# Retention's output projection as seven block products in a written order, with its row and weight sums made during the gates

## The chip, the cores and the metric

One Trainium2 chip, of which the kernel uses one core. The metric is the device time of one execution in microseconds (us), the median of three runs. In the profiled execution TensorE had 0.998 of its full clock granted, so times can be compared across the whole span.

## The reference, cut to what matters

One layer of a backbone over 1024 tokens and 1024 channels, all in float32: a modulated norm, one wide input projection, neighbourhood attention and bidirectional retention side by side, two sigmoid gates that merge the two branches, an output projection, then a gated MLP. The change is in the retention branch's own projection, in the merge and in what stands next to them:

```python
def _ret_output(o, g):
    ...
    return _merge_heads(on) * jax.nn.silu(g)

def _merge(o_na, o_ret, gate_na, gate_ret, w_proj_na, w_proj_ret, w_out):
    merged = jax.nn.sigmoid(gate_na) * (o_na @ w_proj_na) + jax.nn.sigmoid(gate_ret) * (o_ret @ w_proj_ret)
    return merged @ w_out
```

`o_ret` has 1024 tokens and 1024 columns, `w_proj_ret` is 1024 by 1024. The product `o_ret @ w_proj_ret` is what is computed in another way.

## The kernel before, in words

**Three matmuls for one.** Every float32 operand is split into a high and a low part (`split`, L92): ScalarE casts the tile to the high part (L93), VectorE subtracts that from the tile to get the low part (L94). A product is then three matmuls, high by high, high by low and low by high (`mm_a`, `mm3`, L117 to L130, or `open3`, L1420). So each weight tile of 128 by 512 costs one load, one ScalarE cast and one VectorE subtraction before TensorE can use it. Weights are loaded by SyncE's queue into `raw` buffers, of which there are three (L97), and split into `wc` buffers, of which there are six.

**Seven products.** The gate projections, the MLP's up and the MLP's down projection already use Strassen-Winograd's seven products in place of eight (`Seven`, L1424): both operands are cut in 2 by 2 blocks (A11 to A22 for the weights, B11 to B22 for the rows), four sums of each side are made (S1 to S4, T1 to T4), and the seven products are collected in PSUM and combined on VectorE. The sums of the weights come from one of two places: they are made in DRAM, by copies and accumulating DMAs that GpSimd's queue issues long ahead (`block_sums`, L553, pulled a few at a time by `puts`), or by four `tensor_tensor` adds on GpSimd when the unit is loaded (`Seven.load`, L1427). For the up projection `PRE` (L550) is the number of units whose sums are made in DRAM: 8 before. The others, which come later, add on GpSimd.

**The stages around the change,** in the time of the profile: the gates (to about 891 us; class `Gates`, the unit of one head or one merge gate, its steps interleaved by `interleaved`); the retention projection (891.3 to 978.3 us); the output projection `out_proj` (L1707, from 978.3 us), whose eight token tiles multiply the merged rows with `w_out`; and the up projection of the MLP (units `Opening`, `Later` and `Up`).

**The gates leave their rows in DRAM.** For a retention head, `Gates.done` (L1528) takes Silu of the gate, multiplies it with the normed retention output (L1533) and stores the tile to `d_orr` (L1534). For a merge gate it stores the sigmoid to `d_gate` and the gated attention branch to `d_pn`.

**The retention projection** loads the sixteen `orr` tiles (eight of 128 rows for each half of the tokens) and splits them (`orr_load`, `orr_split`). `pret(db, half)` (L1659) then makes one output tile of 128 channels by 512 tokens: 8 k-blocks by 3 matmuls into one PSUM bank `pr`; VectorE multiplies it with the gate (`sg`, L1663, which reads PSUM); GpSimd adds the attention branch (L1664; VectorE for the last `db`); ScalarE and VectorE split the sum into `mh` and `ml` for the output projection. There are 8 `db` by 2 halves, so 16 such tiles and 384 matmuls. After the loop come the loads and splits of `w_out` (`wo`, L1692, and `wx`/`wc`, L1705).

**What sets the order.** All of this stands in code that a scheduler may move: it orders each engine's instructions itself. Inside `with tc.manual_schedule()` the written order holds on each engine.

Of the kernel before, what the change touches and what calls it, by code (L numbers as in the profile page):

```python
# [8 lines left out]
F32 = mybir.dt.float32  # L9
# [31 lines left out]
def tile_hybrid_layer(ctx, tc: tile.TileContext, io, dbg=None):  # L41
# [25 lines left out]
    d_w = dram.tile([NF // 2, 4, P, 512], F32, name="d_w")  # L67

# [481 lines left out]
    NH, EARLY, PRE = NF // 2, 4, 8  # L550
# [25 lines left out]
    def gate_jobs():  # L576
        return weight_jobs(d_g, [io["w_rg"][h] for h in range(RH)] + [io["w_gate"][db] for db in range((NA_FILL + RET_FILL) // 2, KB)])

    def up_jobs():
        return weight_jobs(d_s, [io["w_up"][seq[n]] for n in range(PRE)])  # L580
# [11 lines left out]
    gate_sums, up_sums = block_sums(gate_jobs()), block_sums(up_jobs())  # L592
# [793 lines left out]
    def g_raw(name):  # L1386
        return rr.tile([P, 512], F32, tag="r", bufs=10, name=name)
# [95 lines left out]

    class Gates(Seven):
# [43 lines left out]
        def done(self, b, half, t=None, src=None):  # L1528
            t = self.c[b, half]
            src, n, cs = t if src is None else src, self.n, slice(half * 512, half * 512 + 512)  # L1530
            act.activation(t, src, AF.Silu if self.kind == "ret" else AF.Sigmoid)
            if self.kind == "ret" or b == 0:
                vec.tensor_tensor(t, t, self.o, ALU.mult)  # L1533
                pool.dma_start(d_orr[2 * n + b, :, cs] if self.kind == "ret" else d_pn[n, half], t)  # L1534
            else:
                act.dma_start(d_gate[2 * n + 1, half], t)

# [60 lines left out]
    orr = {}  # L1598

    def orr_load(raw, half, k, pin=late):  # L1600
        pin(sync.dma_start(raw, d_orr[k, :, half * 512 : half * 512 + 512]))
        return half, k, raw

    def orr_split(half, k, raw):
        i, kb = (k // KH if half else 1 - k // KH), k % KH + KH * half
        orr[half, k] = [hxpool.tile([P, 512], F32R, tag=f"{t}{i}{kb}", bufs=1, name="orr") for t in ("high", "low")]
        split(*orr[half, k], raw)

    steps = interleaved(0, len(gu))
    n0, fetched = steps.index((len(gu) - 1, 0)), []  # L1610
    for n, (i, k) in enumerate(steps):
        gu[i].step(k)
        if k in (1, 2, 3):
            puts(up_sums, (gu[i].u3 if k == 3 else gu[i].u2)[:, 0:1], 2)
        if len(fetched) > 1:
            orr_split(*fetched.pop(0))
        if n0 - KH - 1 <= n < n0 - 1:
            fetched.append(orr_load(wpool.tile([P, 512], F32, tag="raw", bufs=3, name="raw"), 0, n - n0 + KH + 1))
        elif n0 < n <= n0 + KH:
            fetched.append(orr_load(g_raw("orw"), 0, n - n0 - 1 + KH))  # L1620

    def pret_load(db):
        return [wload(io["w_pret"][db, i]) for i in range(2)]

    for r in fetched:
        orr_split(*r)
    wp = {0: pret_load(0)}
# [12 lines left out]

    def merge_load(db, halves=(0, 1)):
        for half in halves:
            sg[db, 0, half] = gtile(half, F32, "sg")
            sync.dma_start(sg[db, 0, half], d_pn[db, half])
            sg[db, 1, half] = t = gtile(half, F32, "sg")
            sync.dma_start(t, d_gate[2 * db + 1, half])
            if (db, 1) in spilled:
                act.activation(t, t, AF.Sigmoid)

# [6 lines left out]

    mg = {}

    def pret(db, half):  # L1659
        m = g_ps("pr")  # L1660
        mm_a(m, wp[db], lambda k: orr[half, k][0], lambda k: orr[half, k][1])
        g = sg[db, 1, half]
        vec.tensor_tensor(g, m, g, ALU.mult)  # L1663
        (vec if db == KB - 1 else pool).tensor_tensor(g, g, sg[db, 0, half], ALU.add)  # L1664
# [5 lines left out]
    merge_load(0, (0,))  # L1670
    rows = [orr_load(gtile(1, F32, "orw"), 1, k, lambda ins: ins) for k in range(2 * RH)]
    for r in rows:
        orr_split(*r)
    wp[1] = pret_load(1)
    merge_load(1, (0,))
    for half in range(2):
        if half:
            merge_load(0, (1,))
            merge_load(1, (1,))
        for db in range(2):  # L1680
            pret(db, half)
    for db in range(2, KB):
        wp[db] = pret_load(db)
        merge_load(db)
        if db == 2:
            brow(0, gate1)
        for half in range(2):
            pret(db, half)
    wo = {}
    for kb in range(KB):  # L1690
        t = wop.tile([P, 2, 512], F32R, tag="wo", bufs=KB, name="wo")
        wo[kb, 0] = wload(io["w_out"][0, kb], into=t)  # L1692
# [10 lines left out]
    for kb in (6, 7, 0, 1, 2, 3, 4, 5):  # L1703
        t = (wop if kb >= 6 else op).tile([P, 2, 512], F32R, tag="wx", bufs=2, name="wx") if kb >= 4 else None
        wo[kb, 1] = wload(io["w_out"][1, kb], into=t)  # L1705
# [237 lines left out]

    opening = [Opening(n) for n in range(EARLY)]
    o0, o1, o2, o3 = opening
    xr = None
    for tb in range(NTB):
# [8 lines left out]
        nx = out_proj(tb)  # L1956
# [398 lines left out]
```

## Time and profile before

| what | value |
| --- | --- |
| median of three runs | 1713.74 us (1713.53 to 1713.92) |
| the profiled execution's own time | 1713.59 us |
| its span, first to last instruction | 1711.8 us (1.8 us lie outside it) |
| VectorE busy | 1224.5 us, 72% |
| ScalarE busy | 832.1 us, 49% |
| GpSimd busy | 595.0 us, 35% |

How to read it: the page gives the busy time of each engine over the whole span, and these shares are averages over stages with different limits. So the views that count here are those cut to a stage: busy time by windows, groups of instructions in a window, and the timeline of one engine. DVE is VectorE, ACT ScalarE, POOL GpSimd, PE TensorE, SP SyncE. In a row of the timeline the first number is the start in us, the second the duration; a row with `x2` stands for two instructions run back to back. In a row of a tile the three numbers between slashes are the shortest, median and longest duration in ns.

### The profile page before, as it was taken

What the parts mean: (1) busy time and instruction counts of PE and PEld (TensorE: products, weight loads), DVE (VectorE), ACT (ScalarE), POOL (GpSimd) and SP (SyncE); (2) the same over time, 40 slices, a digit from 0 to 9 for tenths busy, and PEclk for the clock granted to TensorE, in tenths of its full rate; (3) what the DMA queues carried; (4) which work ended last, traced back from release to release, by engine and by line L of the source; (5) the groups of instructions that cost most, each with busy time, mean ns of one, the idle gap of its engine ahead of it and who ended that gap; (6) DMA issues with size and microseconds to landing.
All of it is one profiled execution on the core that took longest, in us unless ns stands there. A gap on an engine that the chain in (4) does not pass through costs nothing.

```text
span 1711.8 us, 25236 instructions
## 1 busy us (share of the span) xinstructions
PE 1696.4 (99%) x8413; PEld 1418.8 (83%) x8413; DVE 1224.5 (72%) x2423; ACT 832.1 (49%) x1749; POOL 595.0 (35%) x783
## 2 busy tenths in 40 slices
PE   9999999999999999999999999999999999999998
PEld 7788888888888887888888888888888888888886
DVE  5777786665787777565564556897899889846756
ACT  6665665553454435353453323654444444634444
POOL 2112324322344443023322111013666567311444
PEclk9999999999999999999999999999999999999999
DMA  9256779952353533899995657878667766998744
GB/s 378 95 147 170 175 202 233 217 132 63 108 145 93 173 62 91 268 309 308 308 288 175 219 175 209 284 228 251 167 169 199 191 186 174 272 312 288 244 157 176
DMA packets 167554, 344.01 MB, mean 201 GB/s; under 512 B 29824, under 2 KB 46752, under 8 KB 160832
## 3 DMA queue, kind: packets, MB, share of 16 engines
q1 hardware_dynamic: 131888, 242.40, 41.6%
q0 software_dynamic: 20928, 85.06, 23.2%
q10 hardware_dynamic: 14608, 14.95, 2.6%
q8 instruction: 66, 1.08, 0.2%
q14 instruction: 64, 0.52, 0.1%
HBM read 267.03 MB, written 140.82 MB: 238 GB/s over the span
## 4 chain that ended last, share of the span: by engine, by line
PE 81%; DMA 5%; issue 5%; DVE 4%; POOL 3%; ACT 1%; SPq 0%; POOLq 0%; ACTq 0%; DVEq 0%
PE u L1417 31%; PE mm L130 4%; PE mm L128 4%; PE mm L129 4%; PE mm L118 4%; PE mm L119 4%; PE mm L117 4%; PE y L1417 2%; PE R L520 2%; PE ptp L502 2%; DMA ur<-in_w_down 2%; PE pr L118 2%; PE pr L117 2%; PE pr L119 2%; DMA ur<-d_a 2%
## 5 line engine op out<-in xcount | busy, mean ns | idle before, releaser
L1417 PE MATMUL u<-T,wc 128*128 128x512 f32 x1056 | 246.4, 389 | 0.3 <-DVE T L94 0.2
L1417 PEld LDWEIGHTS u<-T,wc 128*128 128x128 f32 x1056 | 198.0, 188 | 42.4 <-DVE T L94 0.6
L1417 PE MATMUL y<-wc,ahl 128*128 128x512 f32 (+1 forms) x936 | 210.1, 386 | 0.4 <-DVE wc L94 0.4
L1417 PEld LDWEIGHTS y<-wc,ahl 128*128 128x128 f32 x936 | 174.1, 188 | 36.4 <-DVE wc L94 0.8
L94 DVE TENSOR_TENSOR wc<-ur,wc 128x512 fp32r<-128x512 f32 x171 | 126.8, 745 | 49.0 <-ACT wc L93 49.0
L93 ACT CAST wc<-ur 128x512 fp32r<-128x512 f32 x171 | 105.7, 622 | 110.4 <-PE u L1417 57.1
L118 PE MATMUL mm<-low,wc 128*128 128x512 f32 (+1 forms) x312 | 119.1, 382 | 0.0
L1417 PE MATMUL u<-h2a,wc 128*128 128x512 f32 x504 | 118.3, 389 | 0.0
L1417 PEld LDWEIGHTS u<-h2a,wc 128*128 128x128 f32 x504 | 94.5, 188 | 19.6
L117 PE MATMUL mm<-hx,wc 128*128 128x512 f32 x264 | 107.2, 406 | 0.3 <-ACT hc L231 0.3
L119 PE MATMUL mm<-hx,wc 128*128 128x512 f32 x264 | 104.8, 397 | 0.0
L532 POOL DMA_DIRECT2D d_ona<-rs x32 | 32.5, 1014 | 207.7 <-DVE st L493 55.0
L1417 PE MATMUL u<-hxT,wc 128*128 128x512 f32 x384 | 90.0, 389 | 0.0
L588 POOL COPY pad<-pu 128x1 f32<-128x1 f32 x62 | 39.7, 640 | 143.0 <-DVE pu L1458 107.1
L1417 PEld LDWEIGHTS u<-hxT,wc 128*128 128x128 f32 x384 | 72.1, 188 | 15.0
L130 PE MATMUL mm<-wc,low 128*128 128x512 f32 (+1 forms) x180 | 68.9, 383 | 0.0
L93 ACT CAST wc<-s 128x512 fp32r<-128x512 f32 x56 | 34.9, 623 | 69.6 <-PE u L1417 65.3
L94 DVE TENSOR_TENSOR ahl<-ur,ahl 128x512 fp32r<-128x512 f32 x66 | 52.5, 801 | 22.0 <-ACT ahl L93 21.8
L93 ACT CAST wc<-raw 128x512 fp32r<-128x512 f32 x78 | 48.5, 622 | 39.0 <-PE pr L119 9.8
L94 DVE TENSOR_TENSOR wc<-raw,wc 128x512 fp32r<-128x512 f32 x78 | 57.2, 738 | 11.8 <-ACT wc L93 9.3
L118 PEld LDWEIGHTS mm<-low,wc 128*128 128x128 f32 x312 | 59.1, 190 | 7.2
L93 ACT CAST wc<-wr 128x512 fp32r<-128x512 f32 x56 | 34.7, 622 | 59.4 <-PE u L1417 44.8
(422 smaller groups left out, 4700.0 us busy)
## 6 DMA issues: line engine op xcount, KB each, us to landing
d_a<-at SPq DMA_DIRECT2D x77, 256.0 KB, 5.6
ur<-d_a SPq DMA_DIRECT2D x77, 256.0 KB, 5.3
ur<-in_w_up SPq DMA_DIRECT2D x76, 256.0 KB, 5.3
d_w<-in_w_down POOLq DMA_DIRECT2D x66, 256.0 KB, 6.7
aw<-in_w_ada SPq DMA_DIRECT2D x32, 512.0 KB, 4.4
d_s<-in_w_up POOLq DMA_DIRECT2D x48, 256.0 KB, 6.7
d_a<-d_a POOLq DMA_DIRECT2D x44, 256.0 KB, 7.3
ur<-d_w SPq DMA_DIRECT2D x44, 256.0 KB, 4.3
```

The costliest lines, as they stand in the source:

```text
L93: act.copy(hi, src)
L94: (lo_eng or vec).tensor_tensor(lo, src, hi.bitcast(F32), ALU.subtract)
L117: pe.matmul(out, wh, xh, start=k == 0, stop=False)
L118: pe.matmul(out, wh, xl, start=False, stop=False)
L119: pe.matmul(out, wl, xh, start=False, stop=k == n - 1)
L128: pe.matmul(out, ah, bh, start=first, stop=False)
L129: pe.matmul(out, ah, bl, start=False, stop=False)
L130: pe.matmul(out, al, bh, start=False, stop=last)
L502: pe.transpose(tp[:, c], self.Pm[h][:, c * P : (c + 1) * P], ident)
L520: pe.matmul(R[:, h], self.pair.V[:, g, h].rearrange("p a b -> p (a b)"), self.PT[h][:, c].rearrange("p a b -> p (a b)"), start=c == 0, sto ...
L588: late(pool.tensor_copy(tick, src))
L1417: pe.matmul(out, a, b, start=first and n == 0, stop=last and n == 2, skip_group_check=True)
```

## The change

**Retention's projection becomes seven products** (`PRET`), each for four blocks `n` of 128 output rows, each of 4 k-blocks by 3 matmuls: 7 x 4 x 12 = 336 matmuls in place of 384. The products p are B11 by A11, T2 by S2, B21 by A12, T3 by S3, T4 by A22, T1 by S1 and B22 by S4.

**The stage is written out.** It is now a loop over 29 blocks q inside `manual_schedule`, with product (p, n) = (q // 4, q % 4). Block q issues the loads for block q+3 and beyond, then TensorE's `product(q)`, `evacuated(q - 1)`, the weight split for product q+2, and, where its table names them, a split of a row operand (`XS`), a split of `w_out` (`WO`, `WX`), the sigmoid of a gate, and the split of a merged tile (`merge`). `evacuated` combines the banks on VectorE: for p = 0 a ScalarE copy, for p = 1 and 3 one subtraction, for p = 2 `merged`, for p = 4, 5 and 6 one combination and `merged`. `merged` is VectorE's product with the gate (L1717) and GpSimd's add (L1718), now always on GpSimd.

**The row sums** T1 to T4 are made in the gates (`Gates.rows`): 16 VectorE `tensor_tensor` operations and 4 T1 and 4 T4 stores to a new DRAM tile `d_rt` are new; T2 and T3 stay in the buffers of `row_tile` and no store is needed for them. The four tiles of B12 are no longer stored.

**The weight sums** of `w_pret` are made in DRAM (`pret_jobs`, `d_p`), by 32 DMAs of GpSimd's queue in the first 40 gate steps. To make room, `PRE` falls from 8 to 4: the up units 4 to 7 make their sums with four GpSimd adds each.

**The merged tiles of the second half of the tokens** are split later: `merge(kb, 1)` stands in the loop over `out_proj`. `out_proj(0)` and the last two weight tiles of `w_out` stand in a manual schedule of their own.

```diff
-    NH, EARLY, PRE = NF // 2, 4, 8
+    NH, EARLY, PRE = NF // 2, 4, 4
...
+        def rows(self, b, half, t):
+            i, k = self.n // 2, 2 * (self.n % 2) + b
+            rows[i, half, k] = r = row_tile("low", k) if half and not i else t
+            vec.tensor_tensor(r, t, self.o, ALU.mult)
+            if i or not half:
+                pool.dma_start(d_orr[KH * i + k, :, half * 512 : half * 512 + 512], r)
+            both = (i, 1 - half, k) in rows
+            if i == 0 and both:
+                rows["T1", k] = t1 = row_tile("high", k)
+                vec.tensor_tensor(t1, rows[0, 0, k], rows[0, 1, k], ALU.subtract)
+                pool.dma_start(d_rt[0, k], t1)
+            if i and half:
+                b12, t1 = rows[0, 1, k], rows["T1", k]
+                vec.tensor_tensor(b12, b12, r, ALU.subtract)
+                vec.tensor_tensor(t1, t1, r, ALU.add)
+            if i and both:
+                t4 = gr.tile([P, 512], F32, tag="c", bufs=5, name="t4")
+                vec.tensor_tensor(t4, rows[1, 0, k], rows["T1", k], ALU.subtract)
+                pool.dma_start(d_rt[1, k], t4)
...
-    def pret(db, half):
-        m = g_ps("pr")
-        mm_a(m, wp[db], lambda k: orr[half, k][0], lambda k: orr[half, k][1])
-        g = sg[db, 1, half]
-        vec.tensor_tensor(g, m, g, ALU.mult)
-        (vec if db == KB - 1 else pool).tensor_tensor(g, g, sg[db, 0, half], ALU.add)
-        h_, l_ = gtile(half, F32R, "mh"), gtile(half, F32R, "ml")
-        split(h_, l_, g)
-        mg[db, half] = (h_, l_)
...
+    def merged(db, half, src):
+        s_, g = sg[db, half]
+        vec.tensor_tensor(g, src, g, ALU.mult)
+        pool.tensor_tensor(g, g, s_, ALU.add)
...
+    XS = {q0 + k: (p, k) for p, q0 in ((2, 2), (3, 6), (4, 10), (5, 14), (6, 20)) for k in range(KH)}
+    WO = {2 + kb: kb for kb in range(KB)}
+    WX = {24: (6,), 25: (7,), 26: (0, 1), 27: (2, 3)}
+    WX_LOAD = {22: (6,), 23: (7,), 24: (0, 1), 25: (2,), 26: (3,)}
...
+        elif p == 4:
+            vec.tensor_tensor(p1[n], bank, p1[n], ALU.subtract)
+            merged(n + KH, 0, p1[n])
+        elif p == 5:
+            vec.tensor_tensor(u3[n], u3[n], bank, ALU.subtract)
+            merged(n + KH, 1, u3[n])
+        else:
+            vec.tensor_tensor(u2[n], u2[n], bank, ALU.add)
+            merged(n, 1, u2[n])
...
+        for q in range(NQ + 1):
...
+            if q < NQ:
+                product(q)
+            if q:
+                evacuated(q - 1)
+            if q + 2 < NQ:
+                w_split(*divmod(q + 2, KH))
+            if q in XS:
+                x_split(*XS[q])
+            if q in WO:
+                wo_split(WO[q])
+            for kb in WX.get(q, ()):
+                wo_split(kb, 1)
+            for q0, half in ((8, 0), (24, 1)):
+                if 0 <= q - q0 < KH:
+                    merge_gate(q - q0, half)
+            for q0, b in ((10, 0), (18, KH)):
+                if 0 <= q - q0 < KH:
+                    merge(b + q - q0, 0)
```

**What moves, on VectorE in the projection.** Before, VectorE has these rows for two output tiles of 24 matmuls each: the product with the gate out of the bank `pr`, a weight split (`wc`) and the split of the merged tile (`ml`).

```order
L1663 TENSOR_TENSOR sg_10382<-pr_10416,sg_10382 128x512
L94 TENSOR_TENSOR wc_10619<-raw_10617,wc_10619 128x512
L94 TENSOR_TENSOR ml_10444<-sg_10382,mh_10443 128x512
L1663 TENSOR_TENSOR sg_10459<-pr_10468,sg_10459 128x512
L94 TENSOR_TENSOR ml_10496<-sg_10459,mh_10495 128x512
L94 TENSOR_TENSOR wc_10694<-raw_10692,wc_10694 128x512
```

Now, in blocks 20 and 21, during two products of 12 matmuls each, VectorE has these: the combination out of PSUM (L1782 for p = 4, L1785 for p = 5), the product with the gate, a weight split, a row split (`xop`) for p = 6, and the split of a merged tile.

```order
L1782 TENSOR_TENSOR row_10402<-pr_10488,row_10402 128x512
L1717 TENSOR_TENSOR sg_10755<-row_10402,sg_10755 128x512
L96 TENSOR_TENSOR wc_10890<-raw_10783,wc_10890 128x512
L96 TENSOR_TENSOR xop_10894<-xr_10781,xop_10893 128x512
L96 TENSOR_TENSOR ml_10898<-sg_10728,mh_10897 128x512
L1785 TENSOR_TENSOR row_10685<-row_10685,pr_10285 128x512
L1717 TENSOR_TENSOR sg_10808<-row_10685,sg_10808 128x512
L96 TENSOR_TENSOR wc_10922<-wr_10813,wc_10922 128x512
L96 TENSOR_TENSOR xop_10926<-xr_10811,xop_10925 128x512
L96 TENSOR_TENSOR ml_10930<-sg_10755,mh_10929 128x512
```

So before there are three rows for 24 matmuls, and here five for 12, of which the one at L1717 reads two tiles of SBUF where L1663 read PSUM.

**At the end of the stage,** after the last product, VectorE's rows are the combinations for p = 6 (L1788), the last splits of `w_out` (`wc` is kb 2 and 3 of its second half of the columns, `wx` kb 4 and 5) and, in between, the splits of merged tiles of the second half of the tokens, which `out_proj(4)` needs first.

```order
L1788 TENSOR_TENSOR u2_10501<-u2_10501,pr_10331 128x512
L96 TENSOR_TENSOR ml_11199<-sg_10960,mh_11198 128x512
L1717 TENSOR_TENSOR sg_11018<-u2_10501,sg_11018 128x512
L96 TENSOR_TENSOR wc_11088<-raw_11021,wc_11088 128x512
L96 TENSOR_TENSOR ml_11203<-sg_10988,mh_11202 128x512
L96 TENSOR_TENSOR wc_11091<-raw_11049,wc_11091 128x512
L1788 TENSOR_TENSOR u2_10533<-u2_10533,pr_10360 128x512
L96 TENSOR_TENSOR wx_11124<-raw_11125,wx_11124 128x512
L1717 TENSOR_TENSOR sg_11046<-u2_10533,sg_11046 128x512
L96 TENSOR_TENSOR ml_11274<-sg_11018,mh_11273 128x512
L96 TENSOR_TENSOR wx_11129<-raw_11130,wx_11129 128x512
```

The two `wx` rows, on which the second half of `out_proj(0)` depends, now stand behind the last combinations and behind three `ml` rows that are not needed so soon.

**On GpSimd, where the up projection's first units end** (`zs` are two adds of those units, `pad` a small copy on which the following DMAs wait), the queue was this before:

```order
L1928 TENSOR_TENSOR zs_12139<-zs_12139,pu_12238 128x512
L588 COPY pad_79<-pu_12427 128x1
L560 DMA d_w_72<-in_w_down 16x4096 x2
L1856 DMA d_a_69<-d_a_69 32x2048
L588 COPY pad_79<-pu_12428 128x1
```

and is now this, with the four sums of unit 4 and then of unit 5:

```order
L2053 TENSOR_TENSOR zs_12275<-zs_12275,pu_12374 128x512
L1431 TENSOR_TENSOR s_12674<-ur_12666,ur_12668 128x512
L1432 TENSOR_TENSOR s_12675<-s_12674,ur_12670 128x512
L1433 TENSOR_TENSOR s_12676<-ur_12670,ur_12666 128x512
L1434 TENSOR_TENSOR s_12677<-ur_12672,s_12675 128x512
L593 COPY pad_81<-pu_12563 128x1
L562 DMA d_w_72<-in_w_down 16x4096 x2
L1981 DMA d_a_69<-d_a_69 32x2048
L1431 TENSOR_TENSOR s_12819<-ur_12811,ur_12813 128x512
```

Four adds stand ahead of the first `pad` copy and four ahead of the second, and so ahead of the DMAs behind those.

More of the change, by code (lines that the diff above doesn't have):

```diff
@@ L1482, in interleaved @@
         return [(i, k) for _, i, k in sorted((7 * i + 2 * k, i, k) for i in range(n0, n) for k in range(7))]
+    rows = {}
     class Gates(Seven):
@@ L1613, in tile_hybrid_layer @@
         if k in (1, 2, 3):
[L1614 to L1627, printed above, removed]
+            puts(pret_sums if n < 40 else up_sums, (gu[i].u3 if k == 3 else gu[i].u2)[:, 0:1], 2)
+        if n in marks:
+            m = marks[n]
+            if m < 4:
+                x_load(0, m, lambda: g_raw("xr"))
+            if 0 < m < 5:
+                x_split(0, m - 1)
+            for n_ in {4: (0, 1), 5: (2,)}.get(m, ()):
+                w_load(0, n_)
+            if m > 4:
+                w_split(0, m - 5)
+            if m == 6:
+                for c in range(KH):
+                    x_load(1, c, None)
+                    x_split(1, c)
     gr.release()
@@ L1672, in tile_hybrid_layer, with merge_load @@
[L1672 to L1692, printed above, removed]
+    def merge_load(db, half):
+        sg[db, half] = t = [gtile(half, F32, "sg") for _ in range(2)]
+        sync.dma_start(t[0], d_pn[db, half])
+        sync.dma_start(t[1], d_gate[2 * db + 1, half])
```

137 lines of the change are left out of this document (111 added, 26 removed).

## The prediction

> **What bounds the kernel now.** I read the page first, then the waits of TensorE, then busy time by stage, then the projection's own tile, groups and timelines. The page's span and its first engine row:
>
> ```profile
> span 1711.8 us, 25236 instructions
> ...
> PE 1696.4 (99%) x8413; PEld 1418.8 (83%) x8413; DVE 1224.5 (72%) x2423; ACT 832.1 (49%) x1749; POOL 595.0 (35%) x783
> ```
>
> TensorE is the bound, and its waits (what it waited for, total, times, longest) say how little is lost now:
>
> ```profile
> PE c L201 <- POOL ident masks.py:199: 1.4, 1, 1.4
> ...
> PE y L1417 <- DVE wc L94: 0.4, 1, 0.4
> ...
> PE u L1417 <- DVE T L94: 0.2, 1, 0.2
> ```
>
> No wait is longer than 1.4 us. So a matmul removed is time gained, unless what feeds TensorE falls behind. Busy time by stage (window, its length, then PE, PEld, DVE, ACT, POOL, the clock, DMA share and GB/s): two windows of the gates, two of the projection, two of the up projection.
>
> ```profile
> 740.00:800.00 60.00, 60.00 (x267) 49.66 (x266) 34.09 (x52) 24.88 (x41) 20.33 (x40) 1.00 0.95 306
> 800.00:880.00 80.00, 80.00 (x355) 66.24 (x354) 45.20 (x69) 35.74 (x60) 27.53 (x50) 1.00 0.96 302
> 892.00:935.00 43.00, 43.00 (x191) 35.63 (x190) 22.79 (x32) 17.40 (x30) 10.78 (x8) 1.00 0.62 208
> 935.00:978.00 43.00, 43.00 (x191) 35.59 (x190) 24.91 (x35) 16.68 (x28) 10.09 (x7) 1.00 0.61 194
> 1126.00:1146.00 20.00, 19.95 (x89) 16.20 (x88) 19.11 (x25) 10.27 (x14) 3.60 (x4) 1.00 0.80 266
> 1146.00:1166.00 20.00, 20.00 (x90) 16.57 (x89) 17.81 (x23) 9.80 (x14) 8.09 (x12) 1.00 0.86 261
> ```
>
> VectorE is at 53% and 58% in the projection, but at 96% and 89% in the two windows of the up projection: there is room in the one stage and next to none in the other.
>
> **What is removed.** The projection's first and last group of matmuls, and the first of the output projection behind it:
>
> ```profile
> L117 PE MATMUL pr<-orr,wc x128: 389/389/389, 891.3 to 977.6; 128*128 128x512 f32 x128
> ...
> L119 PE MATMUL pr<-orr,wc x128: 389/389/389, 891.7 to 978.1; 128*128 128x512 f32 x128
> L128 PE MATMUL om<-wo,mh x64: 389/389/476, 978.3 to 1065.1; 128*128 128x512 f32 x64
> ```
>
> 3 x 128 = 384 matmuls from 891.3 to 978.3 are 0.2266 us each (the 389 ns of a row overlap). 48 fewer are **-10.9 us**; a product of 12 lasts 2.72, the 28 of them 76.1 us.
>
> **What VectorE has to do in that time.** Its groups before, with GpSimd's add (columns: busy us, mean ns, idle before and what ended it):
>
> ```profile
> L1664 POOL TENSOR_TENSOR sg<-sg 128x512 f32<-128x512 f32 x14 | 20.3, 1451 | 53.0 <-DVE sg L1663 36.7 <-DMA raw<-in_w_out 4.3 <-ACT wc L93 4.2
> L94 DVE TENSOR_TENSOR wc<-raw,wc 128x512 fp32r<-128x512 f32 x17 | 13.7, 807 | 1.1 <-ACT wc L93 1.1
> L1663 DVE TENSOR_TENSOR sg<-pr,sg 128x512 f32<-128x512 f32 x16 | 11.0, 690 | 14.5 <-PE pr L119 14.4
> L94 DVE TENSOR_TENSOR orr<-orw,orr 128x512 fp32r<-128x512 f32 x8 | 6.5, 826 | 1.8 <-ACT orr L93 1.7
> ```
>
> The same subtraction takes 690 ns or more, and the means of 807 and 826 say that some take much more. The timeline of VectorE shows which, and what a step costs when they follow each other:
>
> ```profile
> 899.19 0.68 DVE L1663 TENSOR_TENSOR sg<-pr,sg 128x512 f32<-128x512 f32 x1
> 899.79 2.38 DVE L94 TENSOR_TENSOR orr<-orw,orr 128x512 fp32r<-128x512 f32 x2
> ...
> 913.25 0.69 DVE L1663 TENSOR_TENSOR sg<-pr,sg 128x512 f32<-128x512 f32 x1 [1.35 <-PE pr L119]
> 913.91 0.69 DVE L94 TENSOR_TENSOR wc<-raw,wc 128x512 fp32r<-128x512 f32 x1
> ```
>
> And GpSimd's add beside the second of these rows:
>
> ```profile
> 899.96 1.66 POOL L1664 TENSOR_TENSOR sg<-sg 128x512 f32<-128x512 f32 x1 [3.11 <-DVE sg L1663]
> ```
>
> Starts lie 0.60 us apart, 0.66 at most (913.25 to 913.91). So four operations are 0.65 + 3 x 0.60 = 2.45 us, five are 3.05. But the pair at 899.79 took 2.38 us where two steps end after 0.60 + 0.69 = 1.29: **an add of GpSimd beside VectorE costs VectorE 1.1 us**. Where VectorE has a backlog the up projection shows the same, first VectorE, then GpSimd:
>
> ```profile
> 1259.30 0.68 DVE L1445 TENSOR_TENSOR uu<-pu,u 128x512 f32<-128x512 f32 x1
> ...
> 1263.24 1.77 DVE L94 TENSOR_TENSOR wc<-s,wc 128x512 fp32r<-128x512 f32 x1
> 1264.94 1.77 DVE L94 TENSOR_TENSOR wc<-ur,wc 128x512 fp32r<-128x512 f32 x1
> ```
>
> ```profile
> 1259.19 1.35 POOL L1426 TENSOR_TENSOR s<-ur 128x512 f32<-128x512 f32 x1 [8.65 <-DVE pu L1464]
> ...
> 1262.20 2.27 POOL L1428 TENSOR_TENSOR s<-ur 128x512 f32<-128x512 f32 x1
> 1264.55 1.62 POOL L1429 TENSOR_TENSOR s<-ur,s 128x512 f32<-128x512 f32 x1
> ```
>
> 1.77 in place of 0.69 is 1.1 again, once per add; the operation at 1259.30, which reads PSUM (`pu`), ran its 0.68 right inside an add. In the projection before, this was free: three operations per 24 matmuls (5.44 us) leave VectorE idle anyway.
>
> Now count the operations block by block from the written order, against 2.72 us of TensorE each. Blocks 0 to 8 have four or fewer and no add: 2.45, in time. Blocks 9 to 12 (p = 2 evacuated) have four and an add, 3.55: VectorE falls back 0.83 each, 3.3 us. Block 13 has four without an add, 14 to 16 have three (1.85): that gives back 0.27 + 3 x 0.87 = 2.9. Blocks 17 to 23 all have an add, with four operations, and five in 20 and 21. VectorE enters them 0.4 us late, and 0.2 later because a product's last matmul ends 389 ns after its start and the next begins after 227. It ends block 23 at 0.6 + 5 x 3.55 + 2 x 4.15 = 26.7 us after product 17 began. Its last operation there is the split of the fourth row tile of B22, which product 24 needs for its last three matmuls, after 7 x 2.72 + 2.26 = 21.3 us. The weight splits run two products ahead, so they give only part of this earlier. **TensorE waits 5.4 us in product 24.** Bounds: at the excess that the groups show per add (17 x 0.117 + 8 x 0.136 = 3.1 us over 14 adds, 0.22) a block of four is 2.67 and there is no wait; at 1.27, the 1.1 and the 0.17 between 899.79 and 899.96, the wait is 7 x 0.17 = 1.2 longer. I take 1.1, since here VectorE has a backlog as at 1263.24.
>
> [...]
>
> **At the end of the projection** the rows for transfers count: the projection's hardware queue (packets, MB, share) and the weights of the output projection, then for comparison the gates' weights.
>
> ```profile
> q1 hardware_dynamic: 9022, 16.68, 59.9%
> ...
> raw<-in_w_out SPq DMA_DIRECT2D x16, 256.0 KB, 2.9
> ```
>
> ```profile
> wr<-in_w_gate SPq DMA_DIRECT2D x8, 256.0 KB, 5.6
> ```
>
> There are three `raw` buffers, so the loads of `w_out`'s second half for kb 4 and 5 wait until the splits of kb 1 and 2 are done, in blocks 26 and 27. From product 17, product 24 ends at 27.4 and product 27 at 35.5; `out_proj(0)` needs kb 5 after 24 + 15 matmuls, 35.5 + 8.8 = 44.3, its low part 0.2 later. VectorE has block 24 and 25 (four operations and an add) from 26.7 to 33.8, block 26 (four) to 37.3; kb 2's split, fourth in block 27, ends 2.45 to 3.55 later, in the middle at 40.4. Then 0.4 for issue, 2.9 to land, 0.6 for the cast and a blocked split of 1.8: 46.1. **That is 1.6 us of waiting**; bounds 0 (nothing blocked there) and 3 (landing 5.6 in place of 2.9, less the slack).
>
> **The gates** get 16 VectorE operations more, 16 x 0.60 = 9.6 us, and 8 stores for 4. VectorE is at 57% there and TensorE has no wait, so 0; uncovered it would be at most these 9.6. The 32 DMAs for `w_pret`'s sums replace 32 of the same kind on the same queue; the DMA share of 0.95 and 0.96 shows transfers near their limit without a wait of TensorE. Splits moved out of the projection and the first row splits stand in the same room: 0.
>
> **The up projection** pays for `PRE` = 4: 16 adds, 16 x 1.1 = 17.6 us of VectorE, and the sums of unit 4 stand behind loads. Nothing in the trace shows adds before 1196 us. I place most after 1146, where 2.2 us per 20 and soon more are idle (17.81 of 20) and weight splits run ahead: **0.3 us**, bounds 0 and the rival below.
>
> **Sum:** -10.9 + 5.4 + 1.6 + 0.3 = -3.6. Against the profiled execution (1713.59, that is 1711.8 and 1.8 outside) that is 1710.0; the median stands 0.15 higher, so 1710.1. What a measurement can tell from no change is 0.2%, 3.4 us: below 1710.3 is faster, above 1717.2 slower. The forecast lies on the lower edge.
>
> **The rivals.**
>
> *VectorE keeps up.* If adds fall beside PSUM readers or in pauses (0.22 each, the first bound), all of -10.9 stays: 1702.8. For it: the split at 913.91 was not blocked. Against it: that one came first and had a pause behind it, and here no pauses are left. With half of both waits it is 1706.3. Chance 0.22.
>
> *The whole add blocks, and the end costs 3.* -10.9 + 6.6 + 3 + 0.3 = -1.0: 1712.7. For it: VectorE's backlog lets an add start first. Against it: at 899.79 the add found VectorE at work. [...] Chance 0.14.
>
> *Transfers bind the projection.* The new stage loads some 89 tiles of 262 KB: 23.3 MB in 76.1 + 5.4 us is 286 GB/s; 16.68 MB at 59.9% of 86 us give 324 at full share, so 88%. Loads are issued three blocks (8.2 us) ahead and took 5.6 in the gates at 0.96, so they arrive in time. Were a landing to pass 8.2 by one block, 2.7 us more: 1712.8. Chance 0.07.
>
> *The other side: the up projection's sums.* If units 4 and 5 make their sums before 1146, VectorE gets 8 x 1.1 = 8.8 us there with 0.9 idle (19.11 of 20): 7.9 us on TensorE, -3.9 + 7.9 = +4.0, so 1717.7. It decides from the point where the splits' lead, a few products of 2.72, is used up. For it: GpSimd is idle there, and nothing but buffers holds these adds back. Against it: those buffers are held by the first units' weights. Chance 0.10.
>
> **How the numbers follow.** Forecast 0.47, its own range 1707.5 to 1712, half of it on each side of 1710.3. Faster by over 0.2%: 0.24 + 0.22 = 0.46. Slower: 0.10, and 0.01 for a wait that no row shows: 0.11. The same: what is left, 0.43. The range 1703.5 to 1714.5 leaves out the last rival and the part of the first that has no wait at all, some 0.2 together, and takes in those at 1712.7 and 1712.8 with 1.7 above them for an uncovered part of the gates' 9.6.
>
> **What would show it.** Right: 336 matmuls with one wait of some 5 us on an `xop` split near the 24th product; splits of 1.8 us in blocks 17 to 23; a second wait of 1 to 2 us on `wx` in the first `om`; none in the gates. Wrong: a stage of 76 us without waits, waits on transfers in it, or waits of TensorE in the first units of the up projection.

## The result and the profile after

The changed kernel took 1726.9 us (median of 6 runs, 1722.42 to 1731.87) against 1713.63 for the kernel before on the same chip: a ratio of 1.0076, with a 95% interval of 1.0057 to 1.0096. It is slower by 13 us; the prediction was 1710.1, with a range up to 1714.5. The profiled execution took 1728.52 us. Its span and first engine row:

```profile
span 1726.8 us, 25317 instructions
...
PE 1695.7 (98%) x8365; PEld 1414.2 (82%) x8365; DVE 1283.1 (74%) x2481; ACT 842.0 (49%) x1777; POOL 633.2 (37%) x805
```

There are 48 matmuls fewer, yet TensorE's busy time fell by 0.7 us and not by 10.9. So some of the matmuls that are left took longer. And TensorE now waits. These are the five largest of its waits that were not there before (what for, total, times, longest):

```profile
PE om L130 <- DVE xn L1844: 3.4, 2, 1.9
PE u L1422 <- DVE pu L1469: 3.3, 2, 2.2
PE pr L1422 <- DVE xop L96: 2.9, 2, 2.6
PE u L1422 <- DVE h2l L2156: 2.2, 1, 2.2
PE pr L1422 <- DVE wc L96: 1.7, 2, 1.2
```

All five are waits for VectorE, in four different stages. The output projection's own matmuls say where the time went; in this row they run from 974.9 to 1065.9 us, before from 978.3 to 1065.1 (by the start of the first and the last):

```profile
L130 PE MATMUL om<-wo,mh x64: 389/390/628, 974.9 to 1065.9; 128*128 128x512 f32 x64
```

TensorE starts it 3.4 us sooner and ends it 0.8 later. Followed matmul by matmul against the kernel before, the changed kernel stands at -3.4 us when the output projection starts, at +0.7 at 993 us, in its second token tile, at +2.5 near its end (1068 us), at +8.7 when the up projection has begun (1098 us), at +14.1 after its second unit of GpSimd sums (1164 us), and at +15.0 at the end. Against the -10.9 of the matmuls removed the losses are thus **7.5 us in the projection, 4.1 at the start of the output projection, 8.0 from its end to the start of the up projection, 5.4 in the first up units and 0.9 behind**. Busy time in windows of the first and the fourth shows two different things:

```profile
935.00:955.00 20.00, 19.44 (x86) 15.77 (x84) 19.83 (x26) 7.18 (x13) 6.98 (x5) 1.00 0.58 204
955.00:965.00 10.00, 5.94 (x22) 3.96 (x23) 9.93 (x11) 3.53 (x6) 4.30 (x3) 1.00 0.62 193
965.00:975.00 10.00, 10.00 (x39) 8.07 (x38) 9.76 (x12) 2.99 (x6) 4.96 (x3) 0.83 0.54 177
...
1126.00:1146.00 20.00, 18.85 (x84) 15.30 (x83) 20.00 (x23) 12.00 (x15) 5.68 (x3) 1.00 0.37 122
```

VectorE is full (19.83 of 20, 9.93 of 10, 20.00 of 20), and TensorE waits beside it. Then, from 965 us, TensorE is busy all the time but runs 39 matmuls in 10 us where it ran 46: the granted clock in that window is 0.83.

**In the projection** VectorE did what was forecast. Its timeline for blocks 22 and 23, the last before the late operand is ready:

```profile
957.88 0.69 DVE L1717 TENSOR_TENSOR sg<-row,sg 128x512 f32<-128x512 f32 x1
958.49 0.69 DVE L96 TENSOR_TENSOR wc<-raw,wc 128x512 fp32r<-128x512 f32 x1
959.09 1.78 DVE L96 TENSOR_TENSOR xop<-xr,xop 128x512 fp32r<-128x512 f32 x1
960.79 0.67 DVE L1785 TENSOR_TENSOR row<-row,pr 128x512 f32<-128x512 f32 x1
961.50 0.69 DVE L1717 TENSOR_TENSOR sg<-row,sg 128x512 f32<-128x512 f32 x1
962.11 0.68 DVE L96 TENSOR_TENSOR wc<-wr,wc 128x512 fp32r<-128x512 f32 x1
962.71 1.76 DVE L96 TENSOR_TENSOR xop<-xr,xop 128x512 fp32r<-128x512 f32 x1
```

A block of four with GpSimd's add takes 3.62 us (from 957.88 to 961.50), with one operation per block slowed from 0.69 to 1.78. TensorE in the same time (start, length, and the wait in brackets):

```profile
955.01 3.06 PE L1422 MATMUL pr<-xop,wc 128*128 128x512 f32 x12 [0.56 <-DVE wc L96]
959.23 1.45 PE L1422 MATMUL pr<-xop,wc 128*128 128x512 f32 x5 [1.16 <-DVE wc L96]
960.92 0.97 PE L1422 MATMUL pr<-xop,wc 128*128 128x512 f32 x3 [0.25 <-DVE xop L96]
964.52 10.55 PE L1422 MATMUL pr<-xop,wc 128*128 128x512 f32 x38 [2.63 <-DVE xop L96]
```

The waits are 0.56 + 1.16 + 0.25 + 2.63 = 4.6 us; the last ends at 964.5, with the split that began at 962.71. The row of 38 matmuls lasts 10.55 us, where 37 steps of 0.2266 and the last one's 0.39 make 8.8. That is 1.8 of the 7.5. The last 1.1 lies in the steps at the four waits, about 0.3 each: the matmul before a wait ends 0.39 us after its start, and the step behind one is 0.34, where a step without a wait is 0.2266.

**At the start of the output projection** its second tile of tokens needs a PSUM bank that VectorE has not emptied. TensorE, then VectorE:

```profile
988.37 0.50 PE L130 MATMUL om<-wo,mh 128*128 128x512 f32 x1 [1.91 <-DVE xn L1844]
...
989.93 0.63 PE L130 MATMUL om<-wo,mh 128*128 128x512 f32 x1
990.36 0.63 PE L131 MATMUL om<-wo,mh 128*128 128x512 f32 x1
```

```profile
984.42 3.29 DVE L96 TENSOR_TENSOR ml<-sg,mh 128x512 fp32r<-128x512 f32 x5
987.63 0.68 DVE L1844 TENSOR_TENSOR xn<-om,gate 128x512 f32<-128x512 f32 x1
```

Five splits that `out_proj(4)` needs first stand ahead of the evacuation. And 1.5 us after the wait the steps are 0.43 us (989.93 to 990.36) in place of 0.227, for eight matmuls.

**From the end of the output projection** VectorE waited 7.8 us for a store of `vo` (a tile that the norm behind the projection makes and that SyncE's queue stores to `d_t`), with an evacuation behind it in its queue:

```profile
1066.88 0.69 DVE L96 TENSOR_TENSOR wu<-raw,wu 128x512 fp32r<-128x512 f32 x1 [7.81 <-DMA d_t<-vo]
1067.49 0.68 DVE L1844 TENSOR_TENSOR xn<-om,gate 128x512 f32<-128x512 f32 x1
```

GpSimd had issued three copies for the up weights' sums some 5 us before that store:

```profile
1053.22 0.82 POOL L558 DMA_DIRECT2D d_s<-in_w_up  x1
1053.81 1.02 POOL L558 DMA_DIRECT2D d_s<-d_s  x1
1054.31 1.32 POOL L558 DMA_DIRECT2D d_s<-in_w_up  x1
```

In the kernel before there was one such copy, and the same wait was half as long:

```profile
1052.57 0.82 POOL L556 DMA_DIRECT2D d_s<-d_s  x1 [0.27 <-issue]
```

```profile
1061.96 0.69 DVE L94 TENSOR_TENSOR wu<-raw,wu 128x512 fp32r<-128x512 f32 x1 [3.74 <-DMA d_t<-vo]
```

From its issue the store took 7.9 us to land in the changed kernel and 4.3 us before.

**In the up projection** a wide operation of VectorE stands beside the first of the new adds (VectorE, then GpSimd, then TensorE):

```profile
1139.44 1.27 DVE L1962 SCALAR_TENSOR_TENSOR at<-uu,cw,at 128x1023 f32<-128x1023 f32 x1
...
1141.24 2.31 DVE L1963 SCALAR_TENSOR_TENSOR at<-uu,cw,at 128x1023 f32<-128x1023 f32 x1
1143.47 0.68 DVE L1469 TENSOR_TENSOR pu<-u,pu 128x512 f32<-128x512 f32 x1
```

```profile
1140.24 2.22 POOL L1431 TENSOR_TENSOR s<-ur 128x512 f32<-128x512 f32 x1 [15.51 <-DMA ur<-in_w_up]
```

```profile
1144.30 5.73 PE L1422 MATMUL u<-T,wc 128*128 128x512 f32 x24 [1.15 <-DVE pu L1469]
```

The operation takes 2.31 us in place of 1.27, the evacuation `pu` behind it is late, and TensorE waits for its bank.

### The profile page after: what moved, and what is told of

It reads as the page before. It is cut to its first block, busy times and chain, and to the rows that moved or that the text cites. A ratio compares the mean times of both kernels' runs of the same rounds, so it can differ in the third digit from the quotient of the medians.

```text
span 1726.8 us, 25317 instructions
## 1 busy us (share of the span) xinstructions
PE 1695.7 (98%) x8365; PEld 1414.2 (82%) x8365; DVE 1283.1 (74%) x2481; ACT 842.0 (49%) x1777; POOL 633.2 (37%) x805
## 4 chain that ended last, share of the span: by engine, by line
PE 50%; DVE 6%; issue 6%; POOL 3%; DMA 3%; ACT 1%; SPq 0%; POOLq 0%; DVEq 0%; ACTq 0%
PE u L1422 30%; PE y L1422 3%; PE pr L1422 2%; PE mm L132 1%; PE mm L131 1%; PE mm L130 1%; DVE wc L96 1%; PE om L130 1%; PE om L132 1%; PE om L131 1%; DMA ur<-d_a 1%; PE pn L119 1%; PE pn L120 1%; PE pn L121 1%; PE mm L1422 1%
## 5 line engine op out<-in xcount | busy, mean ns | idle before, releaser
L96 DVE TENSOR_TENSOR wc<-ur,wc 128x512 fp32r<-128x512 f32 x155 | 118.1, 765 | 45.6 <-ACT wc L95 43.8
L95 ACT CAST wc<-ur 128x512 fp32r<-128x512 f32 x155 | 95.5, 621 | 92.1 <-PE y L1422 44.9
L534 POOL DMA_DIRECT2D d_ona<-rs x32 | 32.7, 1023 | 208.7 <-DVE st L495 65.5
L95 ACT CAST wc<-s 128x512 fp32r<-128x512 f32 x72 | 44.8, 622 | 85.7 <-PE u L1422 83.5
L96 DVE TENSOR_TENSOR wc<-s,wc 128x512 fp32r<-128x512 f32 x72 | 69.3, 963 | 0.7 <-ACT wc L95 0.3
L95 ACT CAST wc<-wr 128x512 fp32r<-128x512 f32 x69 | 42.5, 619 | 53.3 <-PE u L1422 39.4
L1422 PE MATMUL pr<-xop,wc 128*128 128x512 f32 x264 | 63.4, 399 | 4.6 <-DVE xop L96 2.9
```

What stands on the lines that cost most here:

```text
L95: act.copy(hi, src)
L96: (lo_eng or vec).tensor_tensor(lo, src, hi.bitcast(F32), ALU.subtract)
L534: late(pool.dma_start(o, self.rs[HD:P], accum_op=ALU.add))
L1422: pe.matmul(out, a, b, start=first and n == 0, stop=last and n == 2, skip_group_check=True)
```

## The experiments

The theory after the result: each of the four losses has a cause of its own (GpSimd's adds slow VectorE in the projection, 1.78 us for 0.69; the late tiles' splits stand ahead of the evacuations; copies for the up weights' sums hold up a store; GpSimd's sums slow VectorE in the up projection, 2.31 us for 1.27), and a gap of about 2 us or more, as the four waits of 1.9 to 2.6 us in the changed kernel, costs 1.6 us again by a slow clock. The rival: one backlog on VectorE, which shows wherever there is no slack. Each group of runs has its own runs of before: 1714.85, 1715.05, 1714.41 and 1714.85 us for the four groups. Runs of different groups are compared by their ratios to these.

**The sums of the up units alone,** in the kernel before:

```diff
-    NH, EARLY, PRE = NF // 2, 4, 8
+    NH, EARLY, PRE = NF // 2, 4, 4
```

> The kernel before with one part of the change alone: the up units 4 to 7 make their weight sums with GpSimd adds (PRE = 4); the retention projection stays as it was. Theory (every part has its own price, and the adds lock VectorE where it is full): TensorE waits in the first units, between 1130 and 1165 us, as in the changed kernel, where two gaps and a slow clock after the second cost 5.1 us more than before; so 1717 to 1720 us. Rival (these waits are only a consequence of the disturbed stages ahead of them): no new wait between 1130 and 1165, 1713.6 within 0.5 us.

Measured 1716.66 us, ratio 1.0012 (1.0002 to 1.0021). There is a wait where there was none before:

```profile
1135.75 5.72 PE L1417 MATMUL u<-T,wc 128*128 128x512 f32 x24 [2.23 <-DVE pu L1464]
```

So the wait belongs to this edit, and the rival's "no new wait" is wrong. The cost is 1.8 us by the medians, with an interval that only just leaves out no change, and not 3 to 6: one gap, no slow clock behind it. In the changed kernel there are two gaps and a slow clock.

**The merge's adds on VectorE,** in the changed kernel:

```diff
-        pool.tensor_tensor(g, g, s_, ALU.add)
+        vec.tensor_tensor(g, g, s_, ALU.add)
```

> The changed kernel with the 16 adds of the merge on VectorE in place of GpSimd. Theory (an add of GpSimd costs VectorE 1.1 us, its own instruction 0.6): blocks of four become 3.05 in place of 3.55, VectorE ends block 23 at 0.2 + 5 x 3.05 + 2 x 3.65 = 22.8 us after product 17 began, 1.5 us late in place of 5.4, under the gap that slows the clock; of the 7.3 us lost in the projection some 5 come back, and some 2 at the start of the output projection: 1719 to 1722 us. Rival (the count of VectorE's operations is the bound, not the lock): 16 more operations make the stage longer, 7.3 becomes 10 or more: 1729 or above.

Measured 1716.81 us, ratio 1.0019 (1.0008 to 1.003), 10 us less than the changed kernel's median and more than the 5 to 8 us that the theory gave. Its profiled execution was its longest (1724.04), so only its projection is read from it: the output projection starts at 971.1 us in place of 974.9, and of the 4.6 us of waits these are left:

```profile
PE pr L1422 <- DVE xop L96: 1.7, 1, 1.7
PE pr L1422 <- DVE wc L96: 0.8, 1, 0.8
```

VectorE's rows there have no operation of 1.78 us any more:

```profile
957.15 0.69 DVE L1718 TENSOR_TENSOR sg<-sg 128x512 f32<-128x512 f32 x1
957.76 0.68 DVE L96 TENSOR_TENSOR wc<-raw,wc 128x512 fp32r<-128x512 f32 x1
958.36 0.68 DVE L96 TENSOR_TENSOR xop<-xr,xop 128x512 fp32r<-128x512 f32 x1
```

With 16 operations more on VectorE the projection ends 3.8 us sooner: a block of four and the add takes 3.25 us (from 957.76 to 961.01) where it took 3.62 with the add on GpSimd. The slowed operation was the price, not the count. Where the other 6 of the 10 us come from this profile can't show.

**The up weights' sums issued sooner** within the output projection:

```diff
-            puts(up_sums, nx[:, 0:1], 3)
+            puts(up_sums, nx[:, 0:1], 4)
```

> The changed kernel with four in place of three sums of the up weights issued per token tile of the output projection, so that fewer DRAM copies are under way at its end. Theory (the store of vo, which a split of VectorE waits for, lands late behind those copies, and VectorE's queue holds the evacuations): VectorE's wait of 7.8 us on that store falls to about 4, and of the 8.1 us that TensorE loses between 1066 and 1099 some 6 come back: 1720 to 1722 us. Rival (that wait comes from the shifted order of the stage itself): no change beyond the scatter of the changed kernel, 1722 to 1732.

Measured 1725.92 us (ratio 1.0072, 1.0057 to 1.0088): no gain, the rival's figure. VectorE's wait on the store was 8.9 us. The edit did not test what it meant to: four per tile still left the last copy issued at 1052.9 us, behind a wait of GpSimd's queue on the copy before it. The store of `vo` itself now landed in 4.5 us and not 7.9, but SyncE's queue issued it only at 1066.3 us, 9 us after VectorE had made the tile: that queue waited up to 9.6 us for other stores of its own to land (`d_x` and `d_h`). The question stayed open until the sixth run.

**The late tiles' splits behind `out_proj(0)`:**

```diff
         nx = out_proj(0)
+        for kb in range(KB):
+            merge(kb, 1)
```

> The changed kernel with the splits of the merged tiles of the second half of the tokens written behind out_proj(0) inside its manual order, so that they no longer stand ahead of the first evacuations of the output projection. Theory: the wait of TensorE on the evacuation (1.9 us at 988 us, and the slow clock behind it, 4.2 us in all with the wait on wx) goes: 1722 to 1724 us in the profiled execution's frame of 1728.5, that is about 4 us less than the changed kernel on the same chip. Rival (VectorE is simply late by the projection's backlog, so that whatever stands there waits): a gain of under 1 us.

Measured 1722.84 us (ratio 1.0056, 1.0041 to 1.0071), 4.1 less than the changed kernel: the theory's figure. With four and six executions the two intervals overlap, so it is the profile that shows the gain: TensorE has no wait for `xn` at the start of the output projection, and from that start to 1009 us it loses 0.5 us against the kernel before, where the changed kernel lost 4.1.

**Both edits together,** the second's and the fourth's:

```diff
+        vec.tensor_tensor(g, g, s_, ALU.add)
...
         nx = out_proj(0)
+        for kb in range(KB):
+            merge(kb, 1)
```

> The changed kernel with both edits that gained so far: the merge's adds on VectorE and the late tiles' splits behind out_proj(0). Theory: the gains add up, since one acts before and one after the start of the output projection; the run before had 10 us and 4 us, of which the wait on the evacuation at 982 us (3.7 us with the slow clock) is the second's: 1712 to 1715 us. Rival (with VectorE ahead the second edit has nothing left to gain): 1716 to 1718.

Measured 1716.84 us (ratio 1.001, 1.0001 to 1.002): the rival's figure. Against the run of the adds alone nothing was gained. The profile has the projection's waits at 2.5 us and none for `xn` at the start of the output projection, but a new one of 2.1 us later in it, at 1006.6 us: a transpose waits for ScalarE's `h2a`.

**Sums under the projection.** As the fifth run, with one sum of the up weights issued in each of blocks 15 to 28:

```diff
+            if q > 14:
+                puts(up_sums, ..., 1)
```

> The run with both edits, and the up weights' sums issued one by one in blocks 15 to 28 of the projection, so that no more than six are left for the first two token tiles of the output projection. Theory (DRAM copies under way at the end of the output projection delay the store of vo, for which VectorE waits 6.7 to 8.9 us against 3.7 before): that wait falls below 4 us, and the waits of TensorE between 1062 and 1095 us fall from 6 to 8 us to under 1: 5 to 7 us less than the run with both edits. Rival (the wait is on a store that is late by itself): no gain.

Measured 1715.66 us (ratio 1.0009, 1.0 to 1.0018), 1.2 less than the run before it and not 5 to 7. The mechanism is shown all the same: VectorE has no wait on any DMA between 1030 and 1100 us, and TensorE none between 1010 and 1103 us. The store of `vo` landed in 2.0 us. So it did in the first run and the tenth (below), whose copies are all issued before 960 us. But the copies now collide with the last loads of `w_out`:

```profile
PE om L130 <- ACT wx L95: 1.3, 1, 1.3
...
PE om L131 <- DVE wx L96: 0.5, 2, 0.2
```

These and some small ones between 977 and 982 us, with a slow clock behind them, cost 5.0 us there. The last four of these loads took 5.4 to 6.6 us to land, where the fifth run has 2.8 to 4.3. A transfer moved away from one late store made another load late.

**The first half's splits later,** blocks 24 to 27 in place of 18 to 21, on top of the sixth run:

```diff
-            for q0, b in ((10, 0), (18, KH)):
+            for q0, b in ((10, 0), (24, KH)):
```

> The run before, with the splits of the merged tiles kb 4 to 7 of the first half in blocks 24 to 27 in place of 18 to 21. Theory (in blocks 17 to 23 VectorE is the bound: 5 + 2 x 4 + 4 x 5 operations and not 5 + 4 x 6 + 2 x 5 must end there): block 23 ends 0.2 + 3.05 + 2 x 2.45 + 4 x 3.05 = 20.4 us after product 17 began, before the 21.3 at which it is needed, so the waits of TensorE between 950 and 965 us (3.1 us with the adds on VectorE) go, and up to 1 us comes back as a wait at the start of the output projection: 2 to 3 us less than the run before it. Rival (VectorE's work is only moved behind): no gain, the same wait some 20 us later.

Measured 1716.94 us (ratio 1.0009, 1.0 to 1.0019): no gain, the rival's figure. The projection's waits fell to 0.5 us as worked out, but TensorE then waited 2.5 us for `mh` and 1.9 for `xn` at the start of the output projection, with a slow clock after each.

**Gaps made on purpose,** in the kernel before (the added operations leave the values as they are):

```diff
+        for _ in range({2: 1, 3: 3, 5: 9, 6: 15}.get(tb, 0)):
+            l_ = mg[0, half][1][:, ts]
+            vec.scalar_tensor_tensor(l_, done_[0][:, 896:1024], 0.0, l_.bitcast(F32), ALU.mult, ALU.add)
```

> The kernel before with waits of TensorE made on purpose: before the token tiles 2, 3, 5 and 6 of the output projection 1, 3, 9 and 15 small operations of VectorE (a low part plus zero times the tile before) stand between the last evacuation and the next matmuls, so that TensorE waits some 1.5, 2.1, 4 and 6 us. Theory (a gap of over about 2 us is followed by some 8 matmuls at half the clock, which cost 1.6 us): none after the first, one after each of the last two: about 13.6 + 3 to 5 us more than before, 1730 to 1733 us. Rival (the slow clock in the changed kernel had another cause, such as the load of the other engines): 13.6 us more and all matmuls at 227 ns, 1727.

One run, 1739.54 us. The gaps came out larger than planned, since transposes and their VectorE work waited too, so the total says nothing; the rows do. After the first small gap (0.97 us) the steps stay at 0.227. After the largest, 4.91 us, they do not:

```profile
1020.16 0.69 PE L1749 MATMUL tp<-ident,xn 128*128 128x128 f32 x2 [4.91 <-ACT h2a L1760]
...
1021.27 0.63 PE L128 MATMUL om<-wo,mh 128*128 128x512 f32 x1
1021.70 0.63 PE L129 MATMUL om<-wo,mh 128*128 128x512 f32 x1
```

So the slow clock needs nothing of the change but the gap.

**All edits.** The adds of the first half on VectorE; for the second half load, add (GpSimd) and split behind `out_proj(0)`; the sums under the projection; the up units 4 to 7 summed on VectorE:

```diff
+    def add_late(db):
+        g = sg[db, 1][1]
+        s_ = gtile(1, F32, "sg")
+        sync.dma_start(s_, d_pn[db, 1])
+        pool.tensor_tensor(g, g, s_, ALU.add)
...
-            pool.tensor_tensor(self.s1, self.a21, self.a22, ALU.add)
+            self.eng.tensor_tensor(self.s1, self.a21, self.a22, ALU.add)
```

> The changed kernel with what the runs so far point to: the merge's adds on VectorE for the first half of the tokens; for the second half load, add (GpSimd) and split behind out_proj(0); the up weights' sums issued in blocks 15 to 28; the weight sums of the up units 4 to 7 on VectorE (0.6 us each in place of 1.1). Theory: block 23 ends 0.2 + 4 x 3.05 + 3.65 + 2 x 2.45 = 21.0 us after product 17 began, so the projection has no wait; blocks 24 to 27 have four operations and give VectorE's lag back before the output projection, so its evacuations are in time; no wait between 1059 and 1090 us; and the waits in the first up units (5 us) at least halve. The losses left are some 1 to 2 us at the start of the output projection and 2 to 3 in the up projection: 1705 to 1708 us on a chip where before takes 1714 to 1715. Rival (VectorE is so full from the projection to the second up unit that work moved out of one place waits in the next, as in the run with the first half's splits moved): 1713 us or more.

Measured 1723.02 us (ratio 1.0048, 1.0034 to 1.0061). The rival allows this figure (1713 us or more), but the mechanism is another. The projection lost 1 us, and from 1024 to 1157 us there is no wait of over 0.2 us. But two waits in the output projection undid it all, one of 4.2 us at 1007.4 us for ScalarE's `h2a` and this one:

```profile
1020.36 0.80 PE L130 MATMUL om<-wo,mh 128*128 128x512 f32 x1 [11.88 <-DVE xn L1859]
```

```profile
1018.19 1.26 POOL L1727 TENSOR_TENSOR sg<-sg 128x512 f32<-128x512 f32 x1 [3.02 <-DMA sg<-d_pn]
1019.39 0.18 POOL L594 COPY pad<-xn 128x1 f32<-128x1 f32 x1
```

VectorE's write of `xn` at 1019.61 us had waited 3.07 us for GpSimd's small copy of it, and that copy stood behind adds whose loads came late (3.02 us of waiting in the row above).

**The up units' sums on VectorE,** otherwise the first run:

```diff
             if n >= PRE:
+                self.eng = vec if n < 8 else pool
                 return super().load()
```

> The kernel before with the weight sums of the up units 4 to 7 not made in DRAM, as in the first run, but made on VectorE in place of GpSimd. Theory (an add on GpSimd costs a full VectorE 1.1 us, its own 0.6): the one gap of 2.4 us at 1133 us shrinks below 1: within 1 us of before. Rival (any 16 further operations are too much between 1106 and 1166 us, whoever makes them): a gap as before or larger, 1.8 us or more over before.

Measured 1713.31 us (ratio 0.9993, 0.9984 to 1.0002): as fast as before, with no gap there. The 16 operations cost nothing on VectorE and 1.8 us on GpSimd.

**All edits, the late adds on VectorE,** once where the scheduler puts them, once with three of them pinned behind `out_proj(0)`:

```diff
+        for kb in range(max(0, 3 * tb - 3), min(3 * tb, KB)):
+            add_late(kb)
+            merge(kb, 1)
```

> The run with all edits, with the late adds on VectorE instead of GpSimd and load, add and split left to the scheduler in the loop over the token tiles 1 to 3. In that run TensorE lost 19.2 us between 1001 and 1024 us, since the norm's small operation on GpSimd stood behind adds whose loads came late; everything else lost 2.3 us more than before. Theory: without that it is 1723.0 - 19.2, and some 1 us for adds that stand ahead of evacuations: 1704 to 1706 us. Rival (an add that the scheduler puts ahead of the last weight splits makes VectorE wait for a load there): a wait of 2 to 5 us and a slow clock at the start of the output projection: 1708 to 1712.

> The same, with three of the loads issued ahead of out_proj(0) and their adds and splits pinned behind it, so that none stands ahead of a weight split or of the first evacuations. Theory: 1703.5 to 1706 us, at most 1 us from the run with the scheduler's order, or below it if that one waits. Rival (the late loads collide with the output projection's): waits of TensorE between 985 and 1010 us, 1707 or more.

The first took 1710.55 us, ratio 0.9977 (0.9967 to 0.9986): **faster than both kernels** by a little, 0.2% against the one before and not the 9 us expected. The second took 1714.07, ratio 1.0003 (0.9991 to 1.0015). Both are the rivals' figures. What is left in the first is four waits of TensorE between 984 and 1022 us:

```profile
PE om L130 <- DVE xn L1859: 2.8, 2, 1.5
PE tp L1883 <- ACT h2a L1894: 2.7, 2, 2.1
```

VectorE waits 9.3 us there for the late loads (`sg<-d_pn`, four times). In the second, with its loads sooner, these waits of VectorE are 3.4 us, but TensorE waits 5.5 us for `h2a` at 1011.0 us, with a slow clock behind it; why is open. Loading them sooner still was not tried.

## Why the prediction was wrong

- **The matmuls removed, -10.9 us:** right. The cadence is 0.2266 us where the clock is full.
- **VectorE's backlog in the projection, 5.4 us of waiting in product 24:** the mechanism and almost the time were right. The split was to end 26.7 us after product 17 began, at 891.3 + 17 x 2.72 + 26.7 = 964.2; it ended at 964.5. The waits were 4.6. All 16 adds of GpSimd in the projection have one operation of VectorE at 1.8 us beside them, as forecast, and the run with the adds on VectorE has none.
- **What a wait costs, the step that is in none of the sums:** a gap was priced at its length. After four of the gaps the granted clock halves for some eight matmuls (steps of 0.43 us for 0.227), 8 x 0.2 = 1.6 us. Of the 15 us this is 6.4, four times 1.6. The steps at the waits add some 0.3 us each. In the changed kernel waits of 1.9 to 2.6 us were enough, and the slow steps began 0.5 to 1.6 us behind the wait.
- **The end of the projection, 1.6 us on `wx`:** the split ended at 984.3 where 983.6 was forecast; TensorE, later itself, waited only 0.2 us for it. The failed part is what was named in the text as "`ml` rows that are not needed so soon": they were counted against `wx` and not against the evacuation behind them. That wait, with its slow clock, was most of the 4.1; the run with the splits behind shows it.
- **"The 32 DMAs for `w_pret`'s sums replace 32 of the same kind on the same queue",** counted as 0: the largest single miss, 8.0 us. The count was right and the place was not looked at. The up weights' copies now start at 854.8 us and not at 749.6, and run to 1088 us where they ended at 1053: three, not one, are under way when VectorE waits for the store of `vo`. The sixth run moved them away and the waits vanished. What one copy costs a store isn't shown: in the third run the store took 4.5 us with none under way, right behind two loads and a store of the same queue.
- **The up projection, 0.3 us:** it was 5.4. The forecast placed the adds after 1146 us; the first four began at 1140 in a frame 10 us late. The rival on the slower side had this mechanism with 7.9 us and a chance of 0.10. The first and the tenth run show it from both sides.
- **The gates, 0:** right; no wait there.

The sum by its own steps: -10.9 + 4.6 + 0.2 is -6.1 with the waits that were forecast. The other 21 us are the places that were counted as free, the clock, and the steps at the waits.

What stays open: why the edits, each shown in its place in the profile, add up to so little in the median (the fifth to seventh runs lie within 1.3 us of each other), and the scatter of these kernels, 1722.4 to 1731.9 for the changed one. Gaps that have a slow clock behind them in one execution and none in another would make such a scatter, but no run here shows that.

## What to carry to other kernels

Where TensorE has no waits, a part of the work taken from it is worth its time only if every engine that feeds it has slack at each place that the change touches, block by block, for transfers too: what is moved out of a full place can wait in the next, as the splits of the seventh run did (waits of 0.5 us left in the projection, new ones of 2.5 and 1.9 behind it). An add that is moved to GpSimd to relieve VectorE can cost VectorE more than doing it (1.1 against 0.6 us here). And a wait of about 2 us cost some 3.7 us in most cases here, 1.6 of it by the slow clock behind it.

## What the runs showed of the hardware

- **A gap and the clock.** Counted over the starts of TensorE's instructions in all traces of this case, from 880 to 1690 us: of 27 gaps of over 2.2 us from start to start, 22 were followed within 6.5 us by at least five steps of half the clock (0.40 to 0.46 us), and one by four such steps that stand behind a second gap; of 38 gaps between 1.0 and 2.2 us, two were, both in a cluster of gaps. In the changed kernel's own trace seven steps of 0.43 us follow each of the four gaps of 2.30 to 3.03 us, and none follows the four of 1.46 to 1.83. It is not a fixed rule: in the first run a wait of 2.23 us had no slow clock behind it, in the second one of 3.29 us. What set apart the four gaps without a slow clock was not shown; one of the four is followed by only three matmuls before the next wait.
- **What GpSimd's add costs VectorE.** VectorE with a backlog lost 1.1 us to each of the 16 adds of GpSimd in the projection (128x512, 0.68 to 1.78), and up to 1.0 on its 1023-wide operations in the up projection (1.27 to 2.31). GpSimd's own add took 1.6 to 1.7 us in the projection and up to 2.4 in the up projection; in the ninth run, beside a less busy VectorE in the output projection, it took 1.3. The same add on VectorE took 0.6 from start to start.
